# Placing the rows of the moving operands at chosen distances modulo 256 bytes from the weights

## The chip, the cores and the metric

One core of one Trainium2 chip runs the whole program. The metric is the device time of one execution in microseconds (us), the median of several runs. TensorE multiplies a stationary operand (the weights, 128 x 128, loaded by LDWEIGHTS) by a moving operand that streams through it one column at a time; SBUF is the on-chip memory from which both are read, with 128 partitions, and an address in this text is a byte offset within a partition.

## What is computed

One layer of a decoder trunk with two parallel branches, on 256 tokens and 16 learned meta tokens in front of them (L = 272 rows), width 2048, everything in float32:

```python
hn = rmsnorm(h_res, norm_g[l])
p = hn @ w_in[l]            # 2048 x 22528: glu_a, glu_b, conv_gate, q, k, v, ret_gate, merge_a, merge_b
y_a = conformer_branch(glu_a, glu_b, conv_gate, ...)     # GLU, conv of 31 taps, layernorm, gate, @ conv_out
qf = rotate_pairs(q, cos, sin) * (RET_QK_DIM ** -0.5)
kf = rotate_pairs(k, cos, sin)
o = retention_chunkwise(qf, kf, v)                       # 8 heads, decay per head
o = head_groupnorm(o, ret_gn_w[l], ret_gn_b[l])
y_b = (o * jax.nn.silu(ret_gate)) @ ret_out[l]
merged = jax.nn.sigmoid(merge_a) * y_a + jax.nn.sigmoid(merge_b) * y_b
h_res = h_res + merged @ w_out[l]
y = rmsnorm(h_res, final_norm_g)                         # the 16 meta rows are dropped
```

## The kernel before

Each float32 operand of the large products is split into two float32r parts, hi (a rounded copy, made by ScalarE, L50) and lo (what is left, made by VectorE, L51), and a product is the sum of hi x hi, hi x lo and lo x hi. So each block of weights needs three passes of TensorE.

The program is one list of 240 chunks (`stream`, L56), each a block of weights of 128 x 2048, 1 MB in float32. A chunk is loaded by SyncE three chunks ahead (`load`, into one of three buffers raw), split two chunks ahead (`cut`, into one of three buffers whi and one of three wlo, 8192 bytes each) and then used. What is used in which order is the order in which the list is written: for each of 8 heads the GLU gate and value, q, k, the output product of the head before (rout), v and the retention gate; then the merge gate b, the convolution gate, the merge gate a in turn with the convolution's output product (cout), and last the output product (wout). The small steps of a head (scores, turn_values, values, attend, turn_out, gated) hang on marks between chunks.

The chunks of the input product have two forms. `project` (L235) takes all 272 rows: for each of 16 blocks k, the hi weights by the hi row of hn (L239) and by the lo row (L240), and then for each k the lo weights by the hi row (L242). `project_wide` (L245) takes the 256 rows behind the meta tokens: the hi weights by hi and lo row together, as one matmul of 512 columns (L253), and the lo weights by the hi row (L251, 256 columns); its operand a is hn, or s for the chunks of cout. `contract` (L262 on) does the same for rout with z (L265, L266, L268, 256 columns). In the output product (`out_mm`, L664, L665 and L668) the roles change: whi and wlo are the moving operand, with 512 columns (256 for the last quarter's second half), and m is the stationary one. The scores (L392 to L394) and the attention (L476 to L480) are small.

hn is one tile, [128, 16, 2, 272] in float32r: for each k the hi row and then the lo row, 1088 bytes each.

Where a tile lies follows from the order in which the pools give room and from the sizes, each rounded up to 32 bytes: first the pool stage (3 raw, 3 whi, 3 wlo), then pers (par_sb 2432 bytes, cs_sb 2176, idle 64, ident 512, ones 512, nhalf 16, warm 4, u0 and u1 1144 each, hn 34816, fraw/c_sb 16384, fw/yb 16384, row, rcol, pst), then tmp, and above it xin at first, ret for the heads (from sgb, rt0, rt1, kr, khi, klo on), and fin for the last stage (s first). Nothing in the kernel before chooses a place.

Of the kernel before, what the change touches and what calls it, by code (L numbers as in the profile page):

```python
# [23 lines left out]
PAD = TAPS - 1 - NMETA  # L24
HEADS = 8
# [11 lines left out]
def hybrid_kernel(ctx: ExitStack, tc, xt, xrow, xnat, par, fg, cs, dec, win, cout, rout, wout, out):  # L37
# [18 lines left out]
    def stream(src, use):  # L56
        seq.append((src, use))
# [10 lines left out]

    def cut(i, pieces=1):
        if i < len(seq):  # L70
            hi = stage.tile([P, D], F32R, tag="whi", name="whi", bufs=SPLITS)
            lo = stage.tile([P, D], F32R, tag="wlo", name="wlo", bufs=SPLITS)
# [9 lines left out]
    idle = pers.tile([P, KT], F32, name="idle")  # L82
# [23 lines left out]
    hn = pers.tile([P, KT, 2, L], F32R, name="hn")  # L106
    hn_hi, hn_lo = hn[:, :, 0], hn[:, :, 1]
# [15 lines left out]
    nc.gpsimd.memset(pst.bitcast(F32), 0.0)  # L123

# [8 lines left out]
    def pre_norm():  # L133

        raw, hi, lo = [first_raw], [first_w[:, 0]], [first_w[:, 1]]
        for i in range(1, FIRST):
            raw.append(stage.tile([P, D], F32, tag="raw", name="raw", bufs=LOADS))
            hi.append(stage.tile([P, D], F32R, tag="whi", name="whi", bufs=SPLITS))
            lo.append(stage.tile([P, D], F32R, tag="wlo", name="wlo", bufs=SPLITS))
        for i in range(FIRST):  # L140
            parts[i] = (hi[i], lo[i])
        n = KT // CH
# [23 lines left out]
        def normed(k):  # L166
            g = x_sb[:, k, L:L + 1]
            nc.scalar.activation(out=hn_hi[:, k], in_=x_sb[:, k, 0:L], func=AF.Copy, scale=g)
            nc.vector.scalar_tensor_tensor(out=hn_lo[:, k], in0=x_sb[:, k, 0:L], scalar=g,
                                           in1=hn_hi[:, k].bitcast(F32), op0=ALU.mult, op1=ALU.subtract)  # L170

        for c in range(CH):
            w = slice(c * 512, (c + 1) * 512)
# [7 lines left out]
            else:  # L181
                normed(c * n)
                normed(c * n + 1)
                split(raw[0][:, w], hi[0][:, w], lo[0][:, w])
                normed(c * n + 2)
                normed(c * n + 3)
            for i in range(1, FIRST):
                split(raw[i][:, w], hi[i][:, w], lo[i][:, w])
# [46 lines left out]
    def project(acc, hi, lo, ks=range(KT)):  # L235

        for k in ks:
            w = hi[:, k * P:(k + 1) * P]
            nc.tensor.matmul(acc[:, 0:L], lhsT=w, rhs=hn_hi[:, k], start=(k == 0), stop=False)  # L239
            nc.tensor.matmul(acc[:, 0:L], lhsT=w, rhs=hn_lo[:, k], start=False, stop=False)  # L240
        for k in ks:
            nc.tensor.matmul(acc[:, 0:L], lhsT=lo[:, k * P:(k + 1) * P], rhs=hn_hi[:, k],  # L242
                             start=False, stop=(k == KT - 1))

    def project_wide(acc, hi, lo, a):  # L245

        both = acc.rearrange("p (h t) -> p h t", h=2)
        for k in range(KT):
            if k == KT - 1:
                for j in range(KT):  # L250
                    nc.tensor.matmul(acc[:, 0:SEQ], lhsT=lo[:, j * P:(j + 1) * P], rhs=a[:, j, 0],  # L251
                                     start=False, stop=False)
            nc.tensor.matmul(both, lhsT=hi[:, k * P:(k + 1) * P], rhs=a[:, k], start=(k == 0), stop=(k == KT - 1))  # L253
# [19 lines left out]
    def proj_chunk(blk, n, evac):  # L273
        def use(hi, lo, acc=None):
# [33 lines left out]
    def head(h):  # L308
# [12 lines left out]
        def glu(j):  # L321
            def f(acc):
                nc.vector.tensor_tensor(out=u_sb[j][:, PAD:], in0=acc[:, 0:L], in1=s["b", j], op=ALU.mult)
# [57 lines left out]
    def scores(h):  # L381
        s = st[h]
        dec_sb = ret.tile([P, 528], F32, tag="dec", name="dec")
# [26 lines left out]
        p2 = ret.tile([96, 16], F32, tag="p2", name="p2")  # L410
# [475 lines left out]
```

## Time and profile before

| | us |
|---|---|
| median of 3 runs | 1433.21 |
| lowest and highest run | 1432.71 and 1433.38 |
| the profiled execution | 1432.94 |
| its span, first to last instruction | 1431.1 |
| TensorE busy in it (99%) | 1422.0 |
| VectorE busy in it (76%) | 1090.6 |
| ScalarE busy in it (48%) | 691.5 |

The profile records one execution. The span is the time from the first to the last instruction of the program; the rest of the execution's time lies around it. Busy is the time in which at least one instruction of an engine runs. The matmuls of TensorE are pipelined, so their records overlap: one of 272 columns is recorded with some 288 ns, while the next starts some 125 ns after it. Whether a matmul is short is therefore read from the starts, or from a comparison of durations of the same shape, and not from the busy share.

### The profile page before, as it was taken

The page shows a single profiled execution, that of the slowest core. Times are in us where ns is not written, and L with a number is a line of the kernel's source. Part 1 is how long each engine was busy: PE and PEld are TensorE (multiplying, and loading weights), DVE is VectorE, ACT ScalarE, POOL GpSimd, SP SyncE. Part 2 cuts the span into 40 slices and gives each one's busy share as a digit, 9 for nine tenths or more (in the row PEclk, how much of TensorE's full clock was granted, in tenths as well). Part 3 has the DMA queues.
Part 4 walks back from the last instruction along what each step waited for, and adds up shares of the span by engine and source line. Part 5 has one row for each costly group of instructions (what it writes and reads, how often), then busy time and mean ns, then how long its engine had stood idle before and what let it go on. Part 6 is the DMA issues. An engine that isn't in the chain of part 4 may idle for free.

```text
span 1431.1 us, 23353 instructions
## 1 busy us (share of the span) xinstructions
PE 1422.0 (99%) x9648; PEld 1320.7 (92%) x9648; DVE 1090.6 (76%) x1513; ACT 691.5 (48%) x823; POOL 176.0 (12%) x315
## 2 busy tenths in 40 slices
PE   9999999999999999999999999999999999999997
PEld 9999999999999999999999999988988888888886
DVE  6799957986896796699689579776888876666543
ACT  6654545445534534544553454355356654444433
POOL 0032023003203201400320320041000000000000
PEclk9999999999999999999999999999999999999999
DMA  8665556456556655655655564556555555555752
GB/s 319 250 222 170 177 198 200 170 201 205 152 189 200 192 177 191 195 166 203 189 171 202 185 192 168 191 181 196 173 200 176 182 201 180 198 181 183 288 182 84
DMA packets 49467, 274.70 MB, mean 192 GB/s; under 512 B 9136, under 2 KB 9904, under 8 KB 18480
## 3 DMA queue, kind: packets, MB, share of 16 engines
q1 hardware_dynamic: 38352, 258.43, 52.8%
q0 software_dynamic: 9280, 8.93, 3.6%
q10 hardware_dynamic: 1728, 5.83, 1.1%
q8 instruction: 76, 1.25, 0.4%
q14 instruction: 31, 0.25, 0.0%
HBM read 262.15 MB, written 2.10 MB: 185 GB/s over the span
## 4 chain that ended last, share of the span: by engine, by line
PE 97%; DVE 1%; issue 1%; ACT 0%; DMA 0%; POOLq 0%; POOL 0%; DVEq 0%; ACTq 0%
PE ps L253 28%; PE ps L251 14%; PE ps L239 11%; PE ps L240 11%; PE ps L242 11%; PE ps L268 4%; PE ps L266 4%; PE ps L265 4%; PE ps L665 2%; PE ps L668 2%; PE ps L664 2%; DVE wlo L51 0%; PE ps L478 0%; PE ps L476 0%; PE ps L477 0%
## 5 line engine op out<-in xcount | busy, mean ns | idle before, releaser
L51 DVE TENSOR_TENSOR wlo<-raw,whi 128x2048 fp32r<-128x2048 f32 (+2 forms) x246 | 547.5, 2227 | 150.5 <-ACT whi L50 118.0
L50 ACT ACTIVATE whi<-raw 128x2048 fp32r<-128x2048 f32 (+2 forms) x246 | 459.2, 1868 | 263.8 <-PE ps L240 140.6
L253 PE MATMUL ps<-hn,whi 128*128 128x512 f32 x1536 | 380.5, 396 | 0.0
L253 PEld LDWEIGHTS ps<-hn,whi 128*128 128x128 f32 x1536 | 284.6, 189 | 58.8
L239 PE MATMUL ps<-hn,whi 128*128 128x272 f32 x1264 | 319.9, 289 | 0.0
L240 PE MATMUL ps<-hn,whi 128*128 128x272 f32 x1264 | 319.6, 286 | 0.0
L240 PEld LDWEIGHTS ps<-hn,whi 128*128 128x128 f32 x1264 | 237.5, 188 | 1.1
L239 PEld LDWEIGHTS ps<-hn,whi 128*128 128x128 f32 x1264 | 237.2, 188 | 0.3
L303 DVE SCALAR_TENSOR_TENSOR c_sb<-u,par_sb,c_sb 128x256 f32<-128x256 f32 x480 | 206.5, 477 | 1.5
L251 PEld LDWEIGHTS ps<-hn,wlo 128*128 128x128 f32 x1536 | 194.7, 189 | 9.1 <-DVE wlo L51 0.3
L251 PE MATMUL ps<-hn,wlo 128*128 128x256 f32 x1536 | 197.1, 282 | 0.0
L242 PE MATMUL ps<-hn,wlo 128*128 128x272 f32 x1264 | 170.4, 286 | 0.0
L242 PEld LDWEIGHTS ps<-hn,wlo 128*128 128x128 f32 x1264 | 162.1, 188 | 0.0
L258 ACT COPY half<-ps 128x256 f32<-128x256 f32 x112 | 41.3, 369 | 238.3 <-PE ps L253 238.1
L421 POOL DMA_DIRECT2D vy<-vx x128 | 73.6, 583 | 568.9 <-DVE xl L434 525.1
L265 PE MATMUL ps<-zhi,whi 128*128 128x256 f32 x512 | 125.9, 280 | 0.0
L266 PE MATMUL ps<-zlo,whi 128*128 128x256 f32 x512 | 125.9, 280 | 0.0
L266 PEld LDWEIGHTS ps<-zlo,whi 128*128 128x128 f32 x512 | 96.2, 188 | 0.1
L265 PEld LDWEIGHTS ps<-zhi,whi 128*128 128x128 f32 x512 | 96.2, 188 | 0.0
L268 PE MATMUL ps<-zhi,wlo 128*128 128x256 f32 x512 | 80.9, 280 | 0.0
L421 POOL DMA_DIRECT2D oy<-ox x128 | 74.0, 585 | 46.4 <-DVE ox L497 27.2
L268 PEld LDWEIGHTS ps<-zhi,wlo 128*128 128x128 f32 x512 | 69.1, 188 | 0.0
(172 smaller groups left out, 1184.2 us busy)
## 6 DMA issues: line engine op xcount, KB each, us to landing
raw<-in_win_dram SPq DMA_DIRECT2D x173, 1024.0 KB, 4.9
raw<-in_rout_dram SPq DMA_DIRECT2D x32, 1024.0 KB, 4.9
raw<-in_cout_dram SPq DMA_DIRECT2D x16, 1024.0 KB, 4.8
raw<-in_wout_dram SPq DMA_DIRECT2D x16, 1024.0 KB, 4.9
vy<-vx POOLq DMA_DIRECT2D x128, 32.0 KB, 2.7
oy<-ox POOLq DMA_DIRECT2D x128, 32.0 KB, 4.4
dec<-in_dec_dram ACTq DMA_DIRECT2D x8, 264.0 KB, 4.0
raw<-in_win_dram SPq DMA_DIRECT2D x8, 256.0 KB, 6.5
```

What stands on the lines that cost most here:

```text
L50: nc.scalar.activation(out=hi, in_=src, func=AF.Copy)
L51: nc.vector.tensor_tensor(out=lo, in0=src, in1=hi.bitcast(F32), op=ALU.subtract)
L239: nc.tensor.matmul(acc[:, 0:L], lhsT=w, rhs=hn_hi[:, k], start=(k == 0), stop=False)
L240: nc.tensor.matmul(acc[:, 0:L], lhsT=w, rhs=hn_lo[:, k], start=False, stop=False)
L242: nc.tensor.matmul(acc[:, 0:L], lhsT=lo[:, k * P:(k + 1) * P], rhs=hn_hi[:, k], start=False, stop=(k == KT - 1))
L251: nc.tensor.matmul(acc[:, 0:SEQ], lhsT=lo[:, j * P:(j + 1) * P], rhs=a[:, j, 0], start=False, stop=False)
L253: nc.tensor.matmul(both, lhsT=hi[:, k * P:(k + 1) * P], rhs=a[:, k], start=(k == 0), stop=(k == KT - 1))
L265: nc.tensor.matmul(acc, lhsT=hi[:, k, col], rhs=a_hi[:, k], start=(j == 0), stop=False)
L266: nc.tensor.matmul(acc, lhsT=hi[:, k, col], rhs=a_lo[:, k], start=False, stop=False)
L268: nc.tensor.matmul(acc, lhsT=lo[:, k, col], rhs=a_hi[:, k], start=False, stop=(j == n - 1))
L303: nc.vector.scalar_tensor_tensor(out=c, in0=u[:, t:t + SEQ], scalar=w, in1=c, op0=ALU.mult, op1=ALU.add)
L421: nc.gpsimd.dma_start(out=dst(q, a), in_=src(q, a))
```

## The change

The tiles that TensorE reads are laid out anew, so that the byte address of a moving row, less that of the weights, has a chosen remainder modulo 256; the number and shape of the matmuls are as before.

- hn becomes [128, 8, 2, 2, 288]: block k lies at k % 8, hi or lo, k // 8, in rows of 288 elements (1152 bytes), of which 272 are used. `hn_row` and `hn_wide` name a row and a pair of rows.
- whi and wlo have room for two halves of 1024 elements, each followed by 32 unused ones (4224 bytes); wlo has 64 elements more. Chunks of the input product (apart=True) have their second half moved by these 32 elements; other chunks lie in one piece. The lo weights of wide chunks and of cout begin 16 elements (64 bytes) further (first). The split of a chunk is still one instruction on each engine, over two rows of 1024.
- Small tiles move what comes behind them: idle is 32 instead of 16 elements, and gap (16 elements), gap2 (24), and paddings in gs, p2 and vlo1 are new.
- Room is won by sharing: dec takes the place of sgb (one tile for both j), v2 that of qlo; in the last stage u0 and u1 hold csum, vl and the gate, and cs_sb holds vsum, the row of reciprocal deviations and every other sg.

```diff
+ROW = 288
+HALF_W = 1024 + 32
-    def stream(src, use):
-        seq.append((src, use))
+    def stream(src, use, apart=False, first=0):
+
+        seq.append((src, use, apart, first))
...
+    def halved(t, first=0):
+
+        return t[:, first:first + 2 * HALF_W].rearrange("p (h c) -> p h c", h=2)[:, :, 0:D // 2]
+
+    def split_tiles(apart, first):
+        hi = stage.tile([P, 2 * HALF_W], F32R, tag="whi", name="whi", bufs=SPLITS)
+        lo = stage.tile([P, 2 * HALF_W + 64], F32R, tag="wlo", name="wlo", bufs=SPLITS)
+        if not apart:
+            return hi[:, 0:D], lo[:, first:first + D]
+        return halved(hi), halved(lo, first)
+
+    def block(w, k):
+        return w[:, k * P:(k + 1) * P] if len(w.shape) == 2 else w[:, k // 8, k % 8 * P:(k % 8 + 1) * P]
...
-            for c in range(pieces):
-                w = slice(c * D // pieces, (c + 1) * D // pieces)
-                split(raw[:, w], hi[:, w], lo[:, w])
+            if seq[i][2]:
+                raw = raw.rearrange("p (h c) -> p h c", h=2)
+            if pieces == 1:
+                split(raw, hi, lo)
+            else:
+                for c in range(2):
+                    split(raw[:, c], hi[:, c], lo[:, c])
...
-    idle = pers.tile([P, KT], F32, name="idle")
+    idle = pers.tile([P, 32], F32, name="idle")
...
-    hn = pers.tile([P, KT, 2, L], F32R, name="hn")
-    hn_hi, hn_lo = hn[:, :, 0], hn[:, :, 1]
+    hn = pers.tile([P, 8, 2, 2, ROW], F32R, name="hn")
+
+    def hn_row(k, low):
+        return hn[:, k % 8, low, k // 8, 0:L]
+
+    def hn_wide(k):
+        return hn[:, k % 8, :, k // 8, NMETA:L]
+
+    gap = pers.tile([P, 16], F32, name="gap")
+    nc.gpsimd.memset(gap, 0.0)
...
+    gap2 = pers.tile([P, 24], F32, name="gap2")
+    nc.gpsimd.memset(gap2, 0.0)
...
-            w = hi[:, k * P:(k + 1) * P]
-            nc.tensor.matmul(acc[:, 0:L], lhsT=w, rhs=hn_hi[:, k], start=(k == 0), stop=False)
-            nc.tensor.matmul(acc[:, 0:L], lhsT=w, rhs=hn_lo[:, k], start=False, stop=False)
+            w = block(hi, k)
+            nc.tensor.matmul(acc[:, 0:L], lhsT=w, rhs=hn_row(k, 0), start=(k == 0), stop=False)
+            nc.tensor.matmul(acc[:, 0:L], lhsT=w, rhs=hn_row(k, 1), start=False, stop=False)
...
-                project_wide(acc, hi, lo, hn[:, :, :, NMETA:])
+                project_wide(acc, hi, lo, hn_wide)
             return lambda: evac(acc)
-        stream(win[blk], use)
+        stream(win[blk], use, True, 0 if n == L else 16)
...
-                t = ret.tile([P, L], F32, tag="sgb", name="sgb", bufs=2)
-                s["b", j] = t
+                if j == 0:
+                    s["b"] = ret.tile([P, 2, L], F32, tag="sgb", name="sgb")
+                t = s["b"][:, j]
...
-                    s["g"] = ret.tile([P, 4, SEQ], F32, tag="gs", name="gs")
+                    s["g"] = ret.tile([P, 4 * SEQ + 16], F32, tag="gs", name="gs")[:, 0:4 * SEQ].rearrange(
+                        "p (b t) -> p b t", b=4)
...
-        dec_sb = ret.tile([P, 528], F32, tag="dec", name="dec")
+        dec_sb = ret.tile([P, 528], F32, tag="sgb", name="dec")
...
-        p2 = ret.tile([96, 16], F32, tag="p2", name="p2")
+        p2 = ret.tile([96, 48], F32, tag="p2", name="p2")[:, 0:16]
...
-            lo = ret.tile([P, DV], F32R, tag=f"vlo{j}", name=f"vlo{j}")
+            lo = ret.tile([P, DV + 48 * j], F32R, tag=f"vlo{j}", name=f"vlo{j}")[:, 0:DV]
...
-        v2 = ret.tile([96, DV], F32R, tag="v2", name="v2")
+        v2 = ret.tile([96, DV], F32R, tag="qlo", name="v2")
...
-            g = fp.tile([P, SEQ], F32, tag="lng", name="lng", bufs=2)
+            g = u_sb[b % 2][:, 0:SEQ]
...
-            sg = fp.tile([P, SEQ], F32, tag="lns", name="lns", bufs=2)
+            sg = cs_sb[:, 1, 0:SEQ] if b % 2 else fp.tile([P, SEQ], F32, tag="lns", name="lns")
...
-        stream(cout[d], conv_out_use(d))
+        stream(cout[d], conv_out_use(d), first=16)
```

## Rows read from the trace of the kernel before

**Rows 1.** The page: busy time of each engine, and the chain that ended last
```profile
PE 1422.0 (99%) x9648; PEld 1320.7 (92%) x9648; DVE 1090.6 (76%) x1513; ACT 691.5 (48%) x823; POOL 176.0 (12%) x315
...
PE 97%; DVE 1%; issue 1%; ACT 0%; DMA 0%; POOLq 0%; POOL 0%; DVEq 0%; ACTq 0%
```

**Rows 2.** The core: us of its span, mean granted TensorE clock as a share
```profile
core 0: 1431.1 us, clock 0.998
```

**Rows 3.** Waits of TensorE, whole run: us in total, times, longest us
```profile
PE ps L129 <- DVE zeros L121: 1.1, 1, 1.1
PE ps L598 <- DVE vsum L590: 0.3, 1, 0.3
PE ps L240 <- DVE hn L169: 0.2, 1, 0.2
```

**Rows 4.** Timeline of TensorE, narrow chunk: start us, us, what, count
```profile
623.53 0.28 PE L239 MATMUL ps<-hn,whi 128*128 128x272 f32 x1
...
627.52 2.14 PE L242 MATMUL ps<-hn,wlo 128*128 128x272 f32 x16
629.50 0.29 PE L239 MATMUL ps<-hn,whi 128*128 128x272 f32 x1
```

**Rows 5.** Timeline of TensorE, wide chunks, hn and s in turn
```profile
1215.59 3.69 PE L253 MATMUL ps<-hn,whi 128*128 128x512 f32 x15
1219.12 2.05 PE L251 MATMUL ps<-hn,wlo 128*128 128x256 f32 x16
1221.01 0.40 PE L253 MATMUL ps<-hn,whi 128*128 128x512 f32 x1
1221.25 3.66 PE L253 MATMUL ps<-s,whi 128*128 128x512 f32 x15
1224.74 2.03 PE L251 MATMUL ps<-s,wlo 128*128 128x256 f32 x16
1226.61 0.40 PE L253 MATMUL ps<-s,whi 128*128 128x512 f32 x1
```

**Rows 6.** Timeline of TensorE, output product of a head
```profile
410.11 0.28 PE L265 MATMUL ps<-zhi,whi 128*128 128x256 f32 x1
...
411.05 0.63 PE L268 MATMUL ps<-zhi,wlo 128*128 128x256 f32 x4
```

**Rows 7.** Groups by line and shape, whole run: busy us, mean ns, idle before
```profile
L253 PE MATMUL ps<-hn,whi 128*128 128x512 f32 x1536 | 380.5, 396 | 0.0
L239 PE MATMUL ps<-hn,whi 128*128 128x272 f32 x1264 | 319.9, 289 | 0.0
L240 PE MATMUL ps<-hn,whi 128*128 128x272 f32 x1264 | 319.6, 286 | 0.0
L251 PE MATMUL ps<-hn,wlo 128*128 128x256 f32 x1536 | 197.1, 282 | 0.0
L242 PE MATMUL ps<-hn,wlo 128*128 128x272 f32 x1264 | 170.4, 286 | 0.0
L265 PE MATMUL ps<-zhi,whi 128*128 128x256 f32 x512 | 125.9, 280 | 0.0
...
L253 PE MATMUL ps<-s,whi 128*128 128x512 f32 x256 | 64.7, 395 | 0.0
...
L251 PE MATMUL ps<-s,wlo 128*128 128x256 f32 x256 | 32.4, 279 | 0.0
```

**Rows 8.** Four lines of TensorE: count, duration ns min/median/max, first and last start
```profile
L253 PE MATMUL ps<-hn,whi x1536: 388/399/584, 44.1 to 1322.3; 128*128 128x512 f32 x192
...
L239 PE MATMUL ps<-hn,whi x1264: 282/288/372, 8.7 to 922.4; 128*128 128x272 f32 x181
...
L251 PE MATMUL ps<-hn,wlo x1536: 277/282/384, 47.7 to 1322.2; 128*128 128x256 f32 x192
...
L668 PE MATMUL ps<-wlo,m x72: 392/395/398, 1335.6 to 1383.9; 128*128 128x512 f32 x72
```

**Rows 9.** Groups of VectorE, whole run: its splits
```profile
L51 DVE TENSOR_TENSOR wlo<-raw,whi 128x2048 fp32r<-128x2048 f32 x236 | 539.9, 2288 | 148.8 <-ACT whi L50 116.3 <-PE ps L242 28.7 <-ACT vT L353 3.5
```

More of the change, by code (lines that the diff above doesn't have):

```diff
@@ L67, in load @@
                 nc.sync.dma_start(out=raws[i][:, w], in_=seq[i][0][:, w])
+    def halved(t, first=0):
[8 more added lines that the diff above has]
+        return w[:, k * P:(k + 1) * P] if len(w.shape) == 2 else w[:, k // 8, k % 8 * P:(k % 8 + 1) * P]
     def cut(i, pieces=1):
         if i < len(seq):
-            hi = stage.tile([P, D], F32R, tag="whi", name="whi", bufs=SPLITS)
-            lo = stage.tile([P, D], F32R, tag="wlo", name="wlo", bufs=SPLITS)
+            hi, lo = split_tiles(*seq[i][2:])
             raw = raws.pop(i)
-            for c in range(pieces):
-                w = slice(c * D // pieces, (c + 1) * D // pieces)
-                split(raw[:, w], hi[:, w], lo[:, w])
+            if seq[i][2]:
[5 more added lines that the diff above has]
+                    split(raw[:, c], hi[:, c], lo[:, c])
             parts[i] = (hi, lo)
@@ L137, in pre_norm, with quarter, split_quarter @@
             raw.append(stage.tile([P, D], F32, tag="raw", name="raw", bufs=LOADS))
-            hi.append(stage.tile([P, D], F32R, tag="whi", name="whi", bufs=SPLITS))
-            lo.append(stage.tile([P, D], F32R, tag="wlo", name="wlo", bufs=SPLITS))
+            a, b = split_tiles(True, 0)
+            hi.append(a)
+            lo.append(b)
         for i in range(FIRST):
             parts[i] = (hi[i], lo[i])
+        def quarter(w, c):
+            return w[:, c * 512:(c + 1) * 512] if len(w.shape) == 2 else w[:, c // 2, c % 2 * 512:(c % 2 + 1) * 512]
+        def split_quarter(i, c):
+            split(quarter(raw[i], c), quarter(hi[i], c), quarter(lo[i], c))
         n = KT // CH
@@ L183, in pre_norm @@
                 normed(c * n + 1)
-                split(raw[0][:, w], hi[0][:, w], lo[0][:, w])
+                split_quarter(0, c)
                 normed(c * n + 2)
@@ L187, in pre_norm @@
             for i in range(1, FIRST):
-                split(raw[i][:, w], hi[i][:, w], lo[i][:, w])
+                split_quarter(i, c)
     def first_chunks():
@@ L250, in project_wide @@
                 for j in range(KT):
-                    nc.tensor.matmul(acc[:, 0:SEQ], lhsT=lo[:, j * P:(j + 1) * P], rhs=a[:, j, 0],
-                                     start=False, stop=False)
-            nc.tensor.matmul(both, lhsT=hi[:, k * P:(k + 1) * P], rhs=a[:, k], start=(k == 0), stop=(k == KT - 1))
+                    nc.tensor.matmul(acc[:, 0:SEQ], lhsT=block(lo, j), rhs=a(j)[:, 0], start=False, stop=False)
+            nc.tensor.matmul(both, lhsT=block(hi, k), rhs=a(k), start=(k == 0), stop=(k == KT - 1))
     def halves(acc, out):
@@ L568, in ln_sums @@
     def ln_sums():
-        csum = fin["csum"] = fin["pool"].tile([P, SEQ], F32, tag="lng", name="csum", bufs=2)
+        csum = fin["csum"] = u_sb[0][:, 0:SEQ]
         nc.vector.tensor_reduce(out=csum, in_=c_sb.rearrange("p b t -> p t b"), op=ALU.add, axis=mybir.AxisListType.X)
@@ L588, in ln_stats @@
                 nc.vector.tensor_tensor(out=vacc, in0=vacc, in1=sq, op=ALU.add)
-        vsum = fp.tile([P, SEQ], F32, tag="lns", name="vsum", bufs=2)
+        vsum = cs_sb[:, 1, 0:SEQ]
         nc.vector.tensor_reduce(out=vsum, in_=vacc.rearrange("p b t -> p t b"), op=ALU.add, axis=mybir.AxisListType.X)
@@ L602, in ln_rstd @@
         rsqrt_cols(rs, cols, 2, 1.0)
-        vl = fin["vl"] = fp.tile([P, 2, P], F32, tag="lng", name="vl", bufs=2)
+        vl = fin["vl"] = u_sb[1][:, 0:SEQ].rearrange("p (t c) -> p t c", t=2)
         for t in range(2):
@@ L611, in ln_row @@
             nc.tensor.matmul(ps2[:, t * P:(t + 1) * P], lhsT=fin["vl"][:, t], rhs=ident, start=True, stop=True)
-        vrow = fp.tile([P, SEQ], F32, name="vrow")
+        vrow = cs_sb[:, 0, 0:SEQ]
         nc.scalar.copy(out=vrow, in_=ps2[:, 0:SEQ])
```

14 lines of the change are left out of this document (6 added, 8 removed).

## The prediction

> **What bounds the kernel now.** I read the page first: TensorE is busy for 99% of the span, and the chain that ended last is 97% TensorE [rows 1]. The granted clock is 0.998 of the upper of its two levels, 2.4 GHz, over the whole span [rows 2]. TensorE waits for another engine three times, 1.1 us at most [rows 3]. So the time is the number of matmuls times the distance from one start to the next (the pitch), and nothing else. A busy share of 99% does not say whether each matmul is as short as it could be; for that I read starts in the timeline and set them against the columns.
>
> At 2.4 GHz one column takes 0.4167 ns, so 272, 256 and 512 columns are 113.3, 106.7 and 213.3 ns. Measured: 32 narrow matmuls (L239 and L240 in turn) from 623.53 to 627.52 are 3.99 us, a pitch of 124.7 ns, and the 16 of L242 take 1.98 us, 123.8 ns [rows 4]. The wide L253 on hn takes 3.53 us for 15, 235.3 ns; on s 3.49 us, 232.7 ns. L251 on hn takes 1.89 us for 16, 118.1 ns; on s 1.87 us, 116.9 ns [rows 5]. L265 and L266 take 0.94 us for 8, 117.5 ns [rows 6]. Everywhere 9 to 11% above the columns. With the counts of [rows 7] (3792 narrow, 1536 and 256 wide, as many of L251, 512 each of L265, L266 and L268) and the output and attention matmuls, the program sends some 3.08 million columns, 1283 us. TensorE is busy for 1422.0 us [rows 1], so 139 us are not columns (the warm-up and a few small float32 matmuls among them). A layout can win no more than that.
>
> **Where the rows lie.** The weights whi and wlo all start at one place modulo 256, since every buffer is a multiple of 256 bytes; call it 0. (While a matmul streams its row, the weights of the next one are loaded; since all columns of weights stand 512 bytes apart, their place modulo 256 is the same for each k.) Between them and hn lie 8064 bytes of small tiles (31.5 times 256), so hn starts at 128. Its rows are 1088 bytes apart, hi and lo in turn, so the moving row minus weights is, for k even, 128 (hi) and 192 (lo); for k odd, 0 and 64. L239 and L242 thus run at 128 and 0 in turn, L240 at 192 and 64. The wide kinds begin 64 bytes further: their hi rows, and L251, at 192 and 64 in turn. In the same way z lies at 160 and s at 32, both constant. In the output, whi and wlo move and m is loaded: 128 against m0, 224 against m1.
>
> After the change the idle tile is 64 bytes longer and hn starts at 192. Its row of 1152 bytes moves k from 8 on by 128, and the second half of each split weight is moved by 128 too (4224 bytes), so the distance no longer depends on k: 192 for all three narrow lines. hn_wide starts 64 further, so L253 is at 0 for its hi and lo rows; wlo is put 64 further for it, so L251 is at 192. The padding does the same for z (192) and s (0 wide, 192 for L251), and the output comes to 0. In short: every kind of up to 272 columns at 192, every kind of 512 columns at 0.
>
> **What the rows say of a distance.** The plainest pair is hn against s: same lines, same shapes, same weights, neighbouring stretches; the alternating distance costs 2.6 ns on L253 and 1.2 ns on L251, 1.1% each [rows 5]. Among the narrow lines L239 at 0 and 128 has a mean of 289 ns, L240 at 192 and 64 has 286, which I read as 3 ns of pitch [rows 7]. Against it: L242, also at 0 and 128, has 286 as well [rows 7]. And L668 goes from 392 to 398 ns [rows 8] though all its matmuls stand at one distance, so part of the pitch depends on what went before and not on the place.
>
> **The change, part by part.**
> Narrow, 3792: the 1264 of L239 come to L240's 286, 3 x 1264 = 3.8 us. A constant distance in place of an alternating one, by the 1.1% of the wide pair, is 1.4 x 3792 = 5.3 us. Together 9.1 us. Ends: 0, and 6 ns each (the shortest L239 is 282 against a median of 288 [rows 8]), 22.8 us.
> L253 on hn, 1536: I take the pitch on s, 2.6 x 1536 = 4.0 us. No wide matmul of before stands at 0, so the ends are far apart: a gain of 11 ns (shortest 388, median 399 [rows 8]) or 16.9 us, and a loss of 6 ns (3 ns, the price of L239, for each of two rows), 9.2 us. I stay by s because it is the only constant distance in this very form.
> L251 on hn: 1.2 x 1536 = 1.8 us. L265 to L268: from 117.5 to the 116.9 of L251 on s, 0.6 x 1536 = 0.9 us. The wide s, the output and attention: nothing, with ends of 6 ns either way for some 680 matmuls, 4.1 us.
> Sum: 9.1 + 4.0 + 1.8 + 0.9 = 15.8 us.
>
> The rest costs nothing, by what covers it. The splits run over two rows of 1024 in place of one of 2048: same count, same elements, 2288 ns on VectorE [rows 9]. Should the break cost as much as 0.1 us each, that is 24 us on an engine that is busy 76% of the span [rows 1] and on which TensorE hardly waits [rows 3]; with that cover gone it would be 24 us on the path. The two new memsets stand on GpSimd ahead of work that nobody waits for. The shared buffers add waits: dec (DMA on ScalarE's queue) waits for the last read of sgb, which the GLU makes in chunk 3 of a head, and the scores come at chunk 10 or later; v2 waits for the score matmuls, six chunks earlier; the next head's q waits for the attention, four chunks earlier, a chunk being some 5.7 us (1215.59 to 1221.25 [rows 5]). Behind these stand the splits, so a wait of a whole chunk would reach TensorE; none is near. In the last stage u takes the place of a pair of buffers of the same depth. No DMA changes its place in a queue.
>
> The profiled execution took 1432.94 us, 1.8 more than its span of 1431.1, and the median of the three runs is 1433.21; I subtract from that: 1433.2 - 15.8 = 1417.
>
> **The rivals.**
> The place doesn't matter, and the change doesn't do what it says. For it: L668's two durations at one distance, and L242. Against it: hn and s. Time: 1433, within 0.2% (1430 to 1436, about what a measurement of this kernel can tell from no change). The Trainium skill, TensorE: Matmul & The Clock Gate, section "Step-by-step: what each phase is for", speaks for this one: it gives TensorE two independent SBUF read ports and says that loading the next weights takes no read bandwidth from the running matmul. By that rule the sum would be 0; the 1.1% between hn and s does not fit it, but no row shows what the two lines differ in other than place.
>
> A good distance clears more than a little: once every matmul stands well, all run like the shortest of today. From the minima [rows 8]: 6 x 3792 + 11 x 1536 + 5 x 1536 (L251, 277 against 282) = 47.3 us, and the same 2% on the some 350 us of z, s and the output, another 7: 54 us, 1379. For it: these durations occur in today's trace, at distances that are mixed. Against it: s, z and L668 are constant and still 9 to 10% above their columns [rows 5, 6]. The Trainium skill, on the same page, section "Wait — 56ns, not 53.3ns?", gives N / 2.4 + 2.5 ns as the pitch of warm matmuls, 215.8 ns for 512 columns; by it the most to be won would be some 110 us, 1323. No row here comes near that.
>
> Slower: distance 0 is where moving row and weights collide. L239, half of it at 0, is the slowest narrow line [rows 7]. The place is L253, the output and the attention: 2200 matmuls of 512 columns at 6 ns, 13.2 us lost, against 3.8 us that L239 gains: 1433 + 9.4 = 1442. It decides from 3.8 / 2200 = 1.7 ns for each wide matmul.
>
> **How the numbers follow.** A moderate gain has 0.45 (own range 1400 to 1430), no change 0.15, the large gain 0.20, the collision 0.20. Faster by over 0.2%: 0.65; same 0.15; slower 0.20. The range takes in the moderate gain, no change, a little over half of the large gain and half of the collision: 1375 to 1443.
>
> **What would show it.** In the changed trace: L239, L240 and L242 with one mean duration, 286 or less; 32 narrow matmuls in 3.91 us rather than 3.99; 15 of L253 on hn in 3.49, like s; TensorE still without waits. A wide pitch of 240 ns would show the collision, one of 226 the large gain, and unchanged pitches that the place is nothing. Wrong beyond that: a wait of TensorE for the splits or for a shared buffer.

## The result and the profile after

The changed kernel took 1416.14 us (median of four executions) where the kernel before, in the same rounds, took 1432.96: a ratio of 0.9893 with a 95% interval of 0.9863 to 0.9924, so 16.8 us less. The profiled execution took 1416.04 us with a span of 1414.3. One of the four took 1423.06, at a granted clock of 0.996 where the others have 0.998 or 0.999; it was not the profiled one, and the runs "again" and "late" below show what most likely made it long.

The page of the changed kernel (busy time of each engine; the chain that ended last) and its core answer to [rows 1, 2]:

```profile
PE 1404.7 (99%) x9648; PEld 1311.4 (93%) x9648; DVE 1090.0 (77%) x1513; ACT 691.4 (49%) x823; POOL 176.1 (12%) x317
...
PE 95%; DVE 2%; ACT 1%; DMA 1%; issue 1%; POOL 0%; POOLq 0%; DVEq 0%; ACTq 0%
```
```profile
core 0: 1414.3 us, clock 0.998
```

The same 9648 matmuls at the same granted clock keep TensorE busy for 17.3 us less, its weight loads (PEld) for 9.3; the other engines are as busy as before, to 0.6 us. The groups by line and shape of the changed kernel (busy us, mean ns, idle before) answer to [rows 7]. L277, L278 and L280 are the old L239, L240 and L242; L289 and L288 the old L253 and L251; L301 the old L265:

```profile
L289 PE MATMUL ps<-hn,whi 128*128 128x512 f32 x1536 | 374.7, 392 | 0.0
L277 PE MATMUL ps<-hn,whi 128*128 128x272 f32 x1264 | 317.1, 287 | 0.0
L278 PE MATMUL ps<-hn,whi 128*128 128x272 f32 x1264 | 316.7, 287 | 0.0
L288 PE MATMUL ps<-hn,wlo 128*128 128x256 f32 x1536 | 195.8, 280 | 0.0
L280 PE MATMUL ps<-hn,wlo 128*128 128x272 f32 x1264 | 171.1, 287 | 0.0
L301 PE MATMUL ps<-zhi,whi 128*128 128x256 f32 x512 | 123.0, 277 | 0.0
...
L289 PE MATMUL ps<-s,whi 128*128 128x512 f32 x256 | 63.5, 391 | 0.0
...
L288 PE MATMUL ps<-s,wlo 128*128 128x256 f32 x256 | 32.8, 281 | 0.0
```

The wide kinds lost 4 ns of their mean, z lost 3; the old L251 lost 2 on hn and gained 2 on s. Of the narrow lines the one that had 289 lost 2, and the two that had 286 have 287. The timeline of TensorE in the wide chunks of the changed kernel answers to [rows 5]:

```profile
1202.46 3.59 PE L289 MATMUL ps<-hn,whi 128*128 128x512 f32 x15
1205.89 2.04 PE L288 MATMUL ps<-hn,wlo 128*128 128x256 f32 x16
...
1208.01 3.59 PE L289 MATMUL ps<-s,whi 128*128 128x512 f32 x15
1211.43 2.05 PE L288 MATMUL ps<-s,wlo 128*128 128x256 f32 x16
```

Fifteen wide matmuls take 3.43 us on hn (3.53 before) and 3.42 on s (3.49); a chunk takes 5.55 us in place of 5.66. A narrow chunk, same view:

```profile
622.63 0.29 PE L277 MATMUL ps<-hn,whi 128*128 128x272 f32 x1
...
626.60 2.15 PE L280 MATMUL ps<-hn,wlo 128*128 128x272 f32 x16
```

Its 32 take 3.97 us, against 3.99 in [rows 4].

By the distances from start to start of all records of a line, in the two profiled executions (worked out from the records; us, with the mean pitch in ns):

| kind | distance after | before | after | difference |
|---|---|---|---|---|
| narrow, L239 to L277 | 192 | 160.7 (127.2) | 157.1 (124.3) | -3.6 |
| narrow, L240 to L278 | 192 | 156.2 (123.6) | 157.1 (124.3) | +0.9 |
| narrow, L242 to L280 | 192 | 156.5 (123.8) | 157.2 (124.4) | +0.7 |
| wide on hn | 0 | 359.7 (234.2) | 354.3 (230.6) | -5.4 |
| L251 to L288 on hn | 192 | 181.4 (118.1) | 180.0 (117.2) | -1.4 |
| z, three lines | 192 | 180.3 (117.3) | 175.1 (114.0) | -5.2 |
| s, wide and lo | 0, 192 | 89.6 | 88.7 | -0.9 |
| output, 512 columns | 0 | 78.4 | 76.2 | -2.2 |
| all of TensorE | | 1422.2 | 1405.4 | -16.8 |

The rows above the last add up to -17.1; what is left, +0.3, lies in the small matmuls. Among them are the 96 of the output with 256 columns, which now stand at 0 and went from 117.8 to 119.8 ns, 0.2 us.

### The profile page after: what moved, and what is told of

The parts are those of the page before. It is cut to its first block, busy times and chain, and to the rows that moved or that the text cites. A ratio compares the mean times of both kernels' runs of the same rounds, so it can differ in the third digit from the quotient of the medians.

```text
span 1414.3 us, 23358 instructions
## 1 busy us (share of the span) xinstructions
PE 1404.7 (99%) x9648; PEld 1311.4 (93%) x9648; DVE 1090.0 (77%) x1513; ACT 691.4 (49%) x823; POOL 176.1 (12%) x317
## 4 chain that ended last, share of the span: by engine, by line
PE 95%; DVE 2%; ACT 1%; DMA 1%; issue 1%; POOL 0%; POOLq 0%; DVEq 0%; ACTq 0%
PE ps L289 27%; PE ps L288 14%; PE ps L278 11%; PE ps L280 11%; PE ps L277 11%; PE ps L302 4%; PE ps L301 4%; PE ps L304 4%; PE ps L703 2%; PE ps L702 2%; PE ps L706 2%; DVE wlo L54 1%; DMA vy<-vx 0%; ACT whi L53 0%; PE ps L515 0%
## 5 line engine op out<-in xcount | busy, mean ns | idle before, releaser
L289 PE MATMUL ps<-hn,whi 128*128 128x512 f32 x1536 | 374.7, 392 | 0.0
L289 PEld LDWEIGHTS ps<-hn,whi 128*128 128x128 f32 x1536 | 283.1, 188 | 55.7
L277 PE MATMUL ps<-hn,whi 128*128 128x272 f32 x1264 | 317.1, 287 | 0.0
L278 PE MATMUL ps<-hn,whi 128*128 128x272 f32 x1264 | 316.7, 287 | 0.0
L278 PEld LDWEIGHTS ps<-hn,whi 128*128 128x128 f32 x1264 | 238.2, 188 | 1.1
L277 PEld LDWEIGHTS ps<-hn,whi 128*128 128x128 f32 x1264 | 238.2, 188 | 0.3
L288 PEld LDWEIGHTS ps<-hn,wlo 128*128 128x128 f32 x1536 | 194.2, 189 | 7.6 <-DVE wlo L54 0.3
L288 PE MATMUL ps<-hn,wlo 128*128 128x256 f32 x1536 | 195.8, 280 | 0.0
L280 PE MATMUL ps<-hn,wlo 128*128 128x272 f32 x1264 | 171.1, 287 | 0.0
L280 PEld LDWEIGHTS ps<-hn,wlo 128*128 128x128 f32 x1264 | 162.8, 189 | 0.0
L301 PE MATMUL ps<-zhi,whi 128*128 128x256 f32 x512 | 123.0, 277 | 0.0
L302 PE MATMUL ps<-zlo,whi 128*128 128x256 f32 x512 | 123.0, 277 | 0.0
L301 PEld LDWEIGHTS ps<-zhi,whi 128*128 128x128 f32 x512 | 96.3, 188 | 0.0
```

What stands on the lines that cost most here:

```text
L277: nc.tensor.matmul(acc[:, 0:L], lhsT=w, rhs=hn_row(k, 0), start=(k == 0), stop=False)
L278: nc.tensor.matmul(acc[:, 0:L], lhsT=w, rhs=hn_row(k, 1), start=False, stop=False)
L280: nc.tensor.matmul(acc[:, 0:L], lhsT=block(lo, k), rhs=hn_row(k, 0), start=False, stop=(k == KT - 1))
L288: nc.tensor.matmul(acc[:, 0:SEQ], lhsT=block(lo, j), rhs=a(j)[:, 0], start=False, stop=False)
L289: nc.tensor.matmul(both, lhsT=block(hi, k), rhs=a(k), start=(k == 0), stop=(k == KT - 1))
L301: nc.tensor.matmul(acc, lhsT=hi[:, k, col], rhs=a_hi[:, k], start=(j == 0), stop=False)
```

## The experiments

Theory: the remainder modulo 256 of moving row minus loaded weights sets the pitch, and a constant remainder is better than two in turn. Rivals: the place means nothing; the gain comes from another part of the change.

**sweep.** A kernel of matmuls alone, in groups of 64 at one distance; its core, where moving tiles ma to mh start 0, 32, ... 224 bytes further than the weights:

```python
for i in range(64):
    nc.tensor.matmul(ps[:, 0:n], lhsT=w[:, i % 16 * P:i % 16 * P + P], rhs=m[:, at + i % 4 * step:][:, 0:n], ...)
```

> This kernel only streams matmuls and computes nothing of the reference: groups of 64 float32r matmuls, each group with one constant distance of the moving row from the weights (0 to 224 bytes in steps of 32), for 256, 272 and 512 columns, with the weights at two places (even, and odd 64 bytes further) and in two orders; last, 256 columns with only 32 columns of weights. Theory 'the place decides': within each shape the pitch depends on the distance and repeats in both orders; 256 columns at 192 run at about 113 ns, as L301 to L304 do after the change (117 at 160), 512 columns at 0 at about 227 ns (236 or 229/237 elsewhere), 272 columns at 192 at 122 to 124 ns. If distance alone counts, even and odd agree. Theory 'history decides': pitches at one distance differ between the two orders by as much as between distances, 3% or more, and there is no order in the distances. Theory 'the loading of weights is the cause': with 32 columns of weights the pitch falls towards the 106.7 ns of 256 columns at every distance; if the moving stream alone is slow it stays at 113 to 118 ns.

Timeline of TensorE in sweep, part of the second order (one row is one group of 64; the start of the next group, less its own, by 64 is its pitch):

```profile
510.17 7.45 PE L56 MATMUL ps<-mg,even 128*128 128x256 f32 x64
517.45 7.67 PE L56 MATMUL ps<-mf,even 128*128 128x256 f32 x64
...
532.55 7.83 PE L56 MATMUL ps<-md,even 128*128 128x256 f32 x64
540.23 7.70 PE L56 MATMUL ps<-mc,even 128*128 128x256 f32 x64
```
```profile
826.28 14.82 PE L64 MATMUL ps<-mc,even 128*128 128x512 f32 x64
840.94 15.08 PE L64 MATMUL ps<-mb,even 128*128 128x512 f32 x64
855.86 14.69 PE L64 MATMUL ps<-ma,even 128*128 128x512 f32 x64
870.39 15.09 PE L64 MATMUL ps<-mh,odd 128*128 128x512 f32 x64
```

At 192 (mg) 256 columns take 7.28 / 64 = 113.8 ns, at 96 (md) 7.68 / 64 = 120.0. For 512 columns 0 (ma) takes 14.53 / 64 = 227.0, 32 (mb) 233.1, 64 (mc) 229.1. The steady pitches inside the groups, ns:

| columns | 0 | 32 | 64 | 96 | 128 | 160 | 192 | 224 |
|---|---|---|---|---|---|---|---|---|
| 256 | 120.0 | 117.8 | 117.8 | 120.0 | 118.7 | 117.4 | 113.3 | 118.3 |
| 272 | 125.4 | 125.8 | 126.6 | 126.6 | 126.7 | 123.3 | 123.4 | 125.4 |
| 512 | 226.7 | 233.3 | 229.0 | 233.3 | 233.2 | 234.2 | 233.3 | 233.3 |

Both starts of the weights, and both orders of the groups, gave the same table but for two entries, by some 1 ns (256 columns at 32, 512 at 128). At 128 the 512 columns alternate between some 229 and 238 ns in the first order. So the place does matter, up to 6% for 256 columns, and "the place doesn't matter" falls. There is no good distance as such: 0 is the best place of 512 columns and among the worst of 256. And no steady pitch of 256 or 512 columns is shorter than 113.3 or 226.7, which is the columns and a sixteenth (106.7 and 213.3 times 17/16). The Trainium skill, TensorE: Matmul & The Clock Gate, section "Step-by-step: what each phase is for", has weight loads take no read bandwidth from the running matmul. If the two reads didn't meet at all, their distance would not matter; these groups differ in it alone, so here the measurement decides against that.

**z_only.** The kernel before with one tile 32 bytes longer, which moves z from 160 to 192:

```diff
-        p2 = ret.tile([96, 16], F32, tag="p2", name="p2")
+        p2 = ret.tile([96, 24], F32, tag="p2", name="p2")[:, 0:16]
```

> The kernel before with one edit: the tile p2 is 32 bytes longer, so that the z rows of L265 to L268 stand at 192 instead of 160 modulo 256 from the weights (the attention's v tiles move by 32 bytes too). Theory 'the place decides': these 1536 matmuls go from 117.3 ns to the 114.0 ns that they have after the whole change, 1536 x 3.3 = 5.1 us, so 1427.9 us, and all other lines stay. Theory 'history or neighbours decide' (what the chunks before and after do): no more than 1 us, 1432 to 1434 us.

1428.05 us (1427.39 to 1428.43), ratio 0.9965 (0.9953 to 0.9978). The groups by line of z_only:

```profile
L240 PE MATMUL ps<-hn,whi 128*128 128x272 f32 x1264 | 319.7, 286 | 0.0
...
L265 PE MATMUL ps<-zhi,whi 128*128 128x256 f32 x512 | 123.1, 277 | 0.0
```

z goes from 280 ns [rows 7] to 277, its pitches from 180.3 to 175.1 us, and the other lines stay. Eight more floats in one small tile are worth 4.9 us: the plainest proof in the kernel itself (the attention's v tiles move with it, but the small matmuls together changed by less than 0.1 us).

**few.** Matmuls alone again: with 32 columns of weights in place of 128, with weights and rows both moved by 32 bytes ("half"), and with distances in turn.

> Groups of 64 matmuls again, nothing of the reference computed. First 32 columns of weights instead of 128, for 256, 272 and 512 columns at each distance; then all weights, but moved by 32 bytes (half), so that 192 bytes of distance come with a row that starts 32 bytes off a multiple of 64; then distances in turn (128 and 0; 192 and 64; 128, 192, 0, 64) as the kernel before has them. Theory 'moving rows and the loading of weights collide, and what is left is the stream's own': with 32 columns of weights the rows at multiples of 64 bytes come to 17/16 of the column time at nearly every distance (113.3, some 120.4 and 226.7 ns), and none goes below. Theory 'only the distance counts': half at 192 runs at 113.3 ns for 256 columns and half at 0 at 226.7 for 512; if the start of the row counts as well, half stays at 116 to 118 and 232 to 234 ns at every distance. The turns should give what the kernel before has: 118 ns for 256 columns at 192 and 64, 234 to 237 for 512, 125 for 272 in the turn of four.

"half" gave the table of sweep again by distance, so the distance counts and not where a row starts. With 32 columns of weights 256 columns take 113.3 at 0, 64 and 192, 115.6 at 128 and 117.3 to 117.8 at the others: the 120.0 at 0 goes away with most of the weights' columns. But 272 columns then take 122.2 to 124.8, and 512 columns 230.4 to 233.5, at 224 even 240.0, also at 0 (231.7), where all 128 columns gave 226.7. A smaller load is no remedy, and that part of the expectation held for 256 columns only.

Distances in turn, ns, with the mean of their constants from the table of sweep in brackets:

| columns | 128 and 0 | 192 and 64 | 128, 192, 0, 64 |
|---|---|---|---|
| 256 | 118.3 (119.4) | 116.7 (115.6) | 117.5 (117.5) |
| 272 | 125.0 (126.1) | 126.7 (125.0) | 125.0 (125.5) |
| 512 | 230.0 (230.0) | 231.1 (231.2) | 231.7 (230.6) |

Turns run from 1.1 ns below to 1.7 ns above the mean of their constants. So a constant distance is not better as such, and the second half of the theory falls; but neither do turns cost nothing everywhere. Of what was expected of them, only the 125 of 272 columns came out.

**chunks.** Matmuls alone in the kernel's order: 15 wide, 16 lo, one wide, for pairs of distances; and narrow chunks.

> The pattern of a chunk alone, nothing of the reference computed: 15 wide matmuls, 16 of 256 columns, 1 wide, four times for each pair of distances (wide at 0 or 64, the others at 0 to 224); then 32 narrow ones in turn and 16 more, twice for each pair of distances of the hi and the lo row, the last 16 at 192. Theory 'distance alone': with 0 and 192 a wide chunk takes 16 x 226.7 + 16 x 113.3 = 5.44 us, a narrow one at 192 throughout 48 x 123.4 = 5.92 us. Theory 'each change of kind costs a way in': the wide chunk at 0 and 192 takes 5.53 to 5.56 us, as in the changed kernel (11.07 us for two from 1202.46 on), because the first six wide matmuls run at 228 to 239 ns and the 256-column ones stay at 118; then no neighbour in the program is needed to explain what the changed kernel does not reach.

Timeline of TensorE in chunks, wide at 0 (ma) and lo at 192 (mg):

```profile
154.19 3.81 PE L65 MATMUL ps<-ma,whi 128*128 128x512 f32 x16
157.84 2.05 PE L64 MATMUL ps<-mg,wlo 128*128 128x256 f32 x16
159.72 3.81 PE L65 MATMUL ps<-ma,whi 128*128 128x512 f32 x16
```

A chunk takes 159.72 - 154.19 = 5.53 us, as in the changed kernel (5.55), and not the 16 x (226.7 + 113.3) = 5.44 of the steady pitches. The 16 lo take 1.88 us, 117.5 ns, though at 192 sweep has 113.3; and the first wides behind them take 239, 233 and 230 ns before they come down to 226.7. So at one distance a kind has more than one lasting pitch. It is plainest with wide and lo both at 64 (mc), in the same view, where the same chunk comes four times:

```profile
246.95 1.98 PE L64 MATMUL ps<-mc,wlo 128*128 128x256 f32 x16
248.76 3.82 PE L65 MATMUL ps<-mc,whi 128*128 128x512 f32 x16
252.42 2.05 PE L64 MATMUL ps<-mc,wlo 128*128 128x256 f32 x16
254.31 3.84 PE L65 MATMUL ps<-mc,whi 128*128 128x512 f32 x16
```

The 16 lo take 1.81 us (113.3 ns) and 1.89 us (117.8 ns) by turns, with the same instructions at the same distance; from chunk to chunk only the PSUM buffer that is written changes, and what ran before. Over all sixteen pairs a chunk took 5.48 to 5.65 us. The narrow chunk at 192 throughout took 5.92 us, 123.3 ns a matmul, the shortest of its 64 pairs (up to 6.03) and just what "distance alone" had said.

**shift64.** The changed kernel with hn 64 bytes further, s, z and the output where they were; narrow is then at 0, the wide on hn at 64, L251's successor at 0:

```diff
-    idle = pers.tile([P, 32], F32, name="idle")
+    idle = pers.tile([P, 48], F32, name="idle")
...
-    gap = pers.tile([P, 16], F32, name="gap")
-    nc.gpsimd.memset(gap, 0.0)
```

> The changed kernel with one edit: idle is 64 bytes longer and gap is left out, so that hn alone lies 64 bytes further and everything else where it was. The distances become 0 for the narrow lines (192 before the edit), 64 for the wide ones on hn (0) and 0 for L288 on hn (192). Theory 'the distance decides': by the sweep's pitches the narrow lines go from 123.4 to 125.4 (3792 x 2.0 = 7.6 us), the wide ones from 226.7 to 229.0 (1536 x 2.3 = 3.5 us) and L288 from 117.2, as measured after the change, to 120.0 (1536 x 2.8 = 4.3 us): 15.4 us, so 1431.5 us, 1427 to 1434. Theory 'what counts is that the distance is the same for all k' (this layout keeps that): within 2 us of the changed kernel, 1414 to 1418.

1430.56 us (1430.22 to 1430.88), ratio 0.9984 (0.9974 to 0.9993): nearly the whole gain is gone. By pitches narrow lost 5.1 us against the changed kernel, the lo on hn 3.8, the wide nothing, and z, whose distance is as it was, 5.9. Timeline of TensorE in the output product of one head, 12 matmuls from first to last row, in the changed kernel and then in shift64:

```profile
398.79 0.28 PE L301 MATMUL ps<-zhi,whi 128*128 128x256 f32 x1
...
400.15 0.28 PE L301 MATMUL ps<-zhi,whi 128*128 128x256 f32 x1
```
```profile
399.51 0.28 PE L299 MATMUL ps<-zhi,whi 128*128 128x256 f32 x1
...
400.92 0.28 PE L299 MATMUL ps<-zhi,whi 128*128 128x256 f32 x1
```

113.3 ns against 117.5 at one distance: the total came as expected, its parts did not. The layout still keeps one distance for all k, and all else of the change, so neither of these is what made the changed kernel faster.

**no_kink, serp, late_serp.** Where the row's step breaks (block 7 to 8) the distance to the weights already loaded is off for one matmul. no_kink uses blocks 0 to 7 twice in the input product and leaves 8 to 15 out; serp takes the blocks forth and back; late_serp is serp with z's last four reversed too, and with the edit of "late" below.

```diff
-        for k in ks:
-            nc.tensor.matmul(acc[:, 0:L], lhsT=block(lo, k), rhs=hn_row(k, 0), start=False, stop=(k == KT - 1))
+        for k in reversed(ks):
+            nc.tensor.matmul(acc[:, 0:L], lhsT=block(lo, k), rhs=hn_row(k, 0), start=False,
+                             stop=(ks[-1] == KT - 1 and k == ks[0]))
```

> The changed kernel, but the input product uses blocks 0 to 7 of hn and of the weights twice and blocks 8 to 15 not at all (so a part of the product is left out and another counted twice); the number and shape of the matmuls stay. What goes is the step of 128 bytes at block 8: there the weights of block 8 are loaded while the row of block 7 still streams, and for one matmul the distance is 64 instead of 192 (128 instead of 0 for the wide ones). Theory 'each such step throws the stream out for several matmuls': the narrow lines come from 124.3 to the sweep's 123.4 ns (3792 x 0.9 = 3.4 us), the wide ones on hn lose the 233 and 231 ns behind block 7 (10.6 ns x 96 = 1.0 us), L288 stays at 117.7 ns throughout (1536 x 0.5 = 0.8 us more): 3.6 us less than the changed kernel, 1412.5. Theory 'the narrow lines are simply no better at 192 than before, in this kernel': within 1 us of the changed kernel.

> The changed kernel, with the blocks taken forth and back: in the narrow chunks the lo weights run from block 15 to 0, in the wide ones block 0 comes last among the hi weights and the lo weights run from 15 to 0. The same products, in another order. A change of kind then falls between blocks that lie on the same side of the step, and a chunk has two steps of 128 bytes instead of four. Theory 'steps throw the stream out': some 10 ns for each step that goes, two in each of 175 chunks, 3 us: 1413. Theory 'only the way in after a change of kind costs': within 1 us of the changed kernel.

> The late attention and the forth-and-back order of the weights' blocks together, with the last four matmuls of each z group in reverse order too, so that z's history is another one again. Theory (a kind of matmul has two steady pitches at one distance and what runs before decides): narrow 124.0, wide 229.7 ns as in the forth-and-back kernel; if z comes back to 114 ns, 1413.5, if it stays at 117.2, 1418.5. Rival (z's 114 ns hang on the distance alone, and the forth-and-back order harmed z in another way): z stays above 116 whatever its order, 1418.5, and a z of 114 with the slow narrow pitch would speak against the theory.

1417.49, 1418.70 and 1418.78 us. Expected were 1412.5 for no_kink and 1413 for serp: both missed. Against the changed kernel, no_kink: narrow -2.5 us, wide -2.5, but z +5.0 and the lo on hn +1.2. serp: narrow -1.5, wide -1.5, lo +0.9, z +5.0. The breaks do cost some 1.5 to 2.5 us among the narrow matmuls and as much among the wide, but z leaves its short pitch (117.2 ns in all three), though no_kink and serp change nothing in z itself; and another order inside z doesn't bring it back. late_serp doesn't tell whether z hangs on its history or on the order in some other way, only that its distance, 192 in all, is not enough.

**first56.** The lo weights of the wide chunks and of cout begin 224 bytes further in place of 64, so their lo rows stand at 32:

```diff
-        stream(win[blk], use, True, 0 if n == L else 16)
+        stream(win[blk], use, True, 0 if n == L else 56)
...
-        stream(cout[d], conv_out_use(d), first=16)
+        stream(cout[d], conv_out_use(d), first=56)
```

> The changed kernel with one number changed twice: the lo weights of wide chunks and of cout begin 56 elements further instead of 16, so L288 stands at 32 instead of 192. By the sweep of single distances (256 columns: 113.3 ns at 192, 116.7 to 117.8 at 32) this would cost up to 1792 x 4 = 7 us. By the pattern of a chunk (117.7 ns at 192 behind wide matmuls at 0, 116.7 at 32, a chunk of 5.520 against 5.533 us) it gains 13 ns in each of 112 chunks, 1.5 us: 1414.6. So a time below the changed kernel's says that how the stream comes in decides between two steady pitches at 192, and a time of 1419 or more that the distance alone does.

1416.58 us (1415.69 to 1416.72), ratio 0.9884 (0.9868 to 0.9901): as the changed kernel. The lo on hn gained 0.5 us, the wide behind it lost 1.4. Neither branch of the expectation came: by the table of sweep the step from 192 to 32 would have cost up to 7 us, by chunks (5.52 us for this pair, 5.53 for the kernel's) it would have gained 1.5. So for these lo matmuls 192 is worth no more than 32 in the kernel.

**again.** The changed kernel once more.

> The changed kernel once more, beside the three that follow, to have its time on the same chip as theirs: 1415.5 to 1416.3 us. If one of its executions took 1423 us for a reason that lies in it (and not in the machine's moment), such executions come again here.

Its four executions took 1423.83, 1424.21, 1415.46 and 1416.01 us, and the profiled one was the first. Waits of TensorE in again, and its timeline at the place:

```profile
PE ps L518 <- ACT ve L498: 5.5, 1, 5.5
```
```profile
948.23 0.79 PE L518 MATMUL ps<-ve,pe 96*128 96x512 f32 x1 [5.52 <-ACT ve L498]
948.82 0.63 PE L514 MATMUL ps<-vhi,phi 128*128 128x512 f32 x1
949.25 0.63 PE L515 MATMUL ps<-vlo,phi 128*128 128x512 f32 x1
```
Windows of again (stretch, its length, busy us of PE, PEld, DVE, ACT and POOL, granted clock, DMA share, GB/s):
```profile
948.20:954.00 5.80, 5.77 (x15) 4.58 (x16) 5.73 (x8) 2.60 (x3) 0.00 (x0) 0.57 0.55 181
954.00:960.00 6.00, 6.00 (x35) 5.22 (x34) 3.05 (x8) 3.20 (x4) 2.40 (x4) 1.00 0.55 180
```

The attention of the last head (L518) waits 5.5 us for its values (ve is a part of them, copied by ScalarE), and behind the wait the granted clock is 0.57 over 5.8 us, near the lower of its two levels (1.2 and 2.4 GHz): the next matmuls stand 0.43 us apart in place of 0.23. 5.8 us at 0.57 are 2.5 us lost, about the rest of the 7.8 us by which this execution is longer than the one of 1416.04. In the profiled execution of 1416.04 us the same wait is only just missed:

```profile
942.01 0.62 ACT L498 CAST ve<-vlo 32x512 fp32r<-32x512 f32 x1
```
```profile
942.69 0.50 PE L518 MATMUL ps<-ve,pe 96*128 96x512 f32 x1
```

ve is done at 942.63 and L518 starts at 942.69. In the kernel before, the same two:

```profile
950.80 0.62 ACT L460 CAST ve<-vlo 32x512 fp32r<-32x512 f32 x1
```
```profile
953.40 0.40 PE L480 MATMUL ps<-ve,pe 96*128 96x512 f32 x1
```

There ve is done at 951.42 and used at 953.40, a slack of 1.98 us. What used it up stands in the timeline of VectorE, first of the changed kernel, last head,

```profile
901.04 7.59 DVE L608 TENSOR_REDUCE u<-c_sb 128x256 f32<-128x4096 f32 x1
...
910.75 0.86 DVE L442 SCALAR_TENSOR_TENSOR p<-ps,rcol,dec 128x256 f32<-128x256 f32 x2
```
then of the kernel before:
```profile
1017.91 7.55 DVE L570 TENSOR_REDUCE csum<-c_sb 128x256 f32<-128x4096 f32 x1
```

The sum over c_sb for the layernorm of the last stage, 7.6 us on VectorE, ran at 1017.91, behind the heads. The change puts its result in u0, so that it no longer needs the last stage's pool:

```diff
-        csum = fin["csum"] = fin["pool"].tile([P, SEQ], F32, tag="lng", name="csum", bufs=2)
+        csum = fin["csum"] = u_sb[0][:, 0:SEQ]
```

u0 is free earlier, and the sum now stands at 901.04, ahead of the last head's p. The chain that ended last in again runs through just what is queued behind it (start, us, what):

```profile
910.57 2.27 DVE wlo L54
912.84 0.79 DVE p L442 x2
...
915.90 0.68 DVE plo L54
...
916.92 1.92 ACT whi L53
...
925.55 6.33 DMA vy<-vx
...
935.55 5.71 DMA vl<-xl
...
947.56 0.63 ACT ve L498
```

p is late, so plo is; ScalarE's copy of plo holds up the next split of weights, and that the values. From the first wide chunk behind the head's last narrow one to GpSimd's first copy of the values it was 929.04 - 924.60 = 4.44 us before, and is 921.03 - 913.96 = 7.07 in the execution of 1416.04 and about 9 in again, where VectorE reaches the sum 2.0 us later. From there on the copies' own length decides: the slowest of the four of vl lands 3.7 us after its issue in the one and 6.3 in the other. shift64, whose sum also stands early, has 1.40 us of slack in its trace, and none of its ten executions was long; no_kink has 1.10, and one of its four took 1424.27; serp and first56 have 0.24 and 0.05, and none of their four each was long. So the slack in one trace doesn't tell how often the wait comes. The step from the sum to the lost slack is read from the traces; a kernel with the sum back in its old place was not run.

**late and after_five.** The changed kernel with the last head's attention one chunk later, and the changed kernel itself in the same rounds:

```diff
-        for at, f in ((10, scores), (13 if h else 12, turn_values), (16, values), (17, attend), (19, turn_out), (22, gated)):
+        la = 1 if h == HEADS - 1 else 0
+        for at, f in ((10, scores), (13 if h else 12, turn_values), (16, values), (17 + la, attend), (19 + la, turn_out),
+                      (22 + la, gated)):
```

> The changed kernel, with the attention of the last head (its outputs' turn and gating too) one chunk later. Theory (the executions of some 1424 us lose their time at this one place: TensorE waits 5.5 us for the last head's values and then runs some matmuls at half pitch): the wait can't come up, since the values get 5.5 us more, so no execution is over 1420, and the median is 1415.5 to 1417. Rival (the place of the wait is a symptom, and the time is lost wherever a late transfer is first felt): some executions are 1422 to 1425 again, with a wait elsewhere.

> The changed kernel itself, in the same rounds as the one with the late attention, to have the share of the executions of some 1424 us on one chip. Theory: a quarter to a half of them, the others 1415.5 to 1416.5. Rival (chance of the chip alone): none, or also in the kernel before.

late: 1415.48 to 1416.42 us, median 1416.07, ratio 0.9881 (0.9866 to 0.9895). after_five: 1415.71 to 1424.54, median 1416.12, two of six over 1423. Over all runs five of the changed kernel's 14 executions took 1423.1 to 1424.5, none of late's four (nor of late_serp's, which has the same edit); by chance alone four such would come once in six tries, so the count for late is weak. The trace says more. Timelines of ScalarE and of TensorE in late:

```profile
942.25 0.62 ACT L498 CAST ve<-vlo 32x512 fp32r<-32x512 f32 x1
```
```profile
948.66 0.39 PE L518 MATMUL ps<-ve,pe 96*128 96x512 f32 x1
```

ve is done at 942.87 and used at 948.66: 5.79 us of slack where there were 0.06. The values of again, 5.5 us late, would just have been in time. late is the best version here: the changed kernel's short time, without its wait.

## Why the prediction was right, and where its terms were not

The total came out (1417 forecast, 1416.14 measured), by terms that missed in both directions: narrow 9.1 forecast and 2.0 measured, wide on hn 4.0 and 5.4, L251 1.8 and 1.4, z 0.9 and 5.2, s and output nothing and 3.1. That 15.8 came so near to 16.8 is luck: the 7.1 us that narrow lacked were made up by z, output and the wide.

- What bounds the kernel, and that only pitches could change: right. All 16.8 us are in TensorE's starts, at the same granted clock.
- "The 1264 of L239 come to L240's": right, -3.6 us for 3.8, and the plainest case of a duration that stood for a pitch (289 and 286 ns of duration; 127.2 and 123.6 of pitch).
- "A constant distance in place of an alternating one", 5.3 us: the term that failed. L240 and L242 had 123.6 and 123.8 ns in turn, about what 272 columns take at a constant 192 by themselves (123.3 in sweep), so there was little to win; they have 124.3 and 124.4 now, +1.6 us. The breaks at block 8 are part of what keeps them above 123.3: no_kink, without them, has 123.3 to 123.8. That turns are dearer is not so in general (few). Nor do the groups show the 1.1% between hn and s [rows 5] as a price of turns: there 256 columns at 192 and 64 in turn take 116.7 ns, and at the constant 32 of s 116.7 to 117.8. What made hn's 118.1 in the kernel stays open, and the wide row on hn, which takes in two distances at once, no run has by itself.
- L253: the constant distance of s was the nearest row and gave the right size by a wrong reason. Place 0 is worth 233 to 226.7 in steady state; behind each lo run the first wides take longer (a mean of 228.1 in chunks), and the break at block 8 costs more (229.0 in no_kink, which has none), so that 230.6 was left.
- z: mis-sized, 0.6 ns forecast and 3.3 measured. It was taken from L251 on s, at another distance, and from 160 to 192 the 256-column row falls from 117.4 to its lowest, 113.3.
- Output: costed at nothing, but L665 went from 237.4 to 227.0 ns, L668 from 233.2 to 226.6, L664 from 229.5 to 227.1. That L668 had two durations [rows 8] was read as history. In sweep 512 columns at 128, its distance to m0, alternate between some 229 and 238 ns by themselves, in one order of the groups and not in the other; so place and history both have a part in it, and at place 0 the two durations are gone.
- The rivals. "Place doesn't matter": against it sweep and z_only. "Collision at 0": for 512 columns the reverse holds. For 256 it exists (120.0); the change puts only the 96 output matmuls of 256 columns there, against the prediction's "every kind of up to 272 columns at 192", and they lost 0.2 us. "All as short as the shortest": output and z nearly came to their 17/16, 226.7 and 113.3; narrow, wide and lo did not, since their pitch also hangs on what ran before, and for hn on the breaks at block 8. The pitch of N / 2.4 + 2.5 ns from the Trainium skill (TensorE: Matmul & The Clock Gate, section "Wait — 56ns, not 53.3ns?") would be 215.8 for 512 columns; no group of these float32r matmuls came under 226.7.
- "The rest costs nothing": the splits did (2287 ns for 2288 in [rows 9]). The shared buffers did not in five of 14 executions. The prediction looked for waits that sharing adds; it did not ask which instruction sharing sets free to move ahead, and named u0 only as a pair of the same depth.

Of the signs named: one mean for the three narrow lines, yes, but 287 and not 286 or less; 3.97 us for 32, not 3.91; 3.43 for 15 wide, better than 3.49; no waits of TensorE, not always.

## What to carry to other kernels

Measure the pitch of each shape over distances modulo 256 in a kernel of matmuls alone before laying anything out: the best distance of 512 columns was a bad one for 256, and padding one small tile was worth 4.9 us. Then judge a layout in the kernel itself by the sums of pitches for each line, since what runs before can undo a good distance elsewhere. And where a buffer is shared or moved, look for the instruction that its freedom lets run earlier, and for what now queues behind it.

## What the runs showed that was not expected

- For 256 float32r columns the pitch goes from 113.3 to 120.0 ns with nothing changed but the distance between moving row and weights, and in no group under 17/16 of the columns' own time.
- At one distance there are two lasting pitches (113.3 and 117.5 for z at 192), and edits elsewhere in the program switch between them: 5 us of the kernel. What picks one stays open.
- Loading a quarter of the weights' columns cures 256 columns at distance 0 (113.3) and harms 512 there (231.7 for 226.7).
- A wait of 5.5 us on TensorE cost 7.8: the rest went to a granted clock of 0.57 over the next 5.8 us.
